# First loads over three queues and first splits held behind the front, in a conditioned short-convolution layer on one Trainium2 core

## The chip, the core and the metric

The kernel runs on one core of a Trainium2 chip. Its time is the device time of one execution in microseconds (us); lower is better. The core has TensorE (PE, with its weight loads shown as PEld), VectorE (DVE), ScalarE (ACT), GpSimd (POOL) and SyncE (SP). Each engine works through its own instructions in order. Transfers are issued by an engine's instructions onto that engine's queue and are carried by 16 DMA engines.

## The reference

One layer is computed on x of 256 tokens by 2048 features, in float32, conditioned by a vector c.

```python
h = rmsnorm(x, norm_g)                         # x * rsqrt(mean(x*x) + 1e-6) * g
mod = silu(c) @ ada_w + ada_b                  # ada_w: 2048 x 6144
shift, scale, gate = split(mod, 3)
h = h * (1 + scale) + shift
b_gate, c_gate, v, g = split(h @ w_in, 4)      # w_in: 2048 x 16384
u = causal_depthwise_conv(c_gate * v, conv_w)  # 3 taps per channel
y = (b_gate * u * silu(g)) @ w_out             # w_out: 4096 x 2048
x = x + gate * y
out = rmsnorm(x, final_g)
```

## The kernel before

Features lie on the partitions. Every large product is done in three float32r products: each operand is split into a rounded part (`hi`, a cast by ScalarE) and the remainder (`lo`, a subtraction by VectorE), and hi*hi, hi*lo and lo*hi are summed.

The program has a **front**, whose order is written out by hand (`in_order` ties each instruction to the one before it on its engine), and a **body**, which the tile framework's scheduler orders by its own timeline of the program (`schedule_with_timeline_sim=True`). Where no tie holds, the scheduler may also put instructions of the body between those of the front. That concerns above all the loads on SP's queue.

The front:

- x is loaded in four tiles of 512 KB, `x_84` and `x_85` (left and right half of the first 128 tokens), `x_86` and `x_87` (of the other 128). Four small loads bring the rows of c, norm_g, ada_b and conv_w; PE turns them into columns (`tp_v`, line 240).
- ScalarE squares the first 128 tokens (line 275), VectorE the others (line 278); from the sums comes `rstd`, with which ScalarE scales x (line 300). PE turns the scaled x (`tp_x`, line 306) and ScalarE copies it to `xs`.
- For the first two of the 16 feature tiles, shift and scale come first. `first_ada` loads their columns of ada_w, 4 MB in pieces `at` of 4, 4, 4, 2, 1 and 1 of the 16 rows of blocks (k); each piece is two transfers, one for shift and one for scale. These pieces borrow the buffers of `lo` and `hi` in turn, three of each. VectorE multiplies each k by silu(c) and adds (`gv`, lines 362 and 364), except the k in `ON_PE`, which PE sums directly (`sum0_of`, line 350). At the end PE sums `gv` over its partitions (`sum0(None, ...)`, line 350), VectorE forms `scale` and `shift` (lines 391 to 393), ScalarE and VectorE write the first two tiles of `hT` (`features`, lines 328 to 332), and the products of `raw0` (512 KB of w_in, two transfers, line 188) begin.
- `idle(n, ...)` issues `IDLE[n]` products without use on PE at fixed places of the front.

The body of the first stage runs two new feature tiles against 1 MB pieces `raw_s` of w_in (line 525, the first is 512 KB), each split by line 338 (`hi`) and line 339 (`lo`) and followed by 48 products on PE (line 466). Three buffers `raw` hold raw0 and the pieces. Between them, `ada_piece` loads the ada_w columns of the later feature tiles in pieces of two transfers of 256 KB (`at`, line 435, four buffers); a group of two feature tiles takes eight such pieces.

A load also waits for the eighth load ahead of it: the framework gives the transfers of SP and ACT eight semaphores (`DMAHW0` to `DMAHW7`) in turn, and a semaphore is used again when the transfer that had it has landed. Transfers of GpSimd have semaphores of their own.

Of the kernel before, what the change touches and what calls it, by code (L numbers as in the profile page):

```python
# [11 lines left out]
ALU = mybir.AluOpType  # L12

P = 128
# [114 lines left out]
def short_conv_layer(ctx: ExitStack, tc: tile.TileContext, x, c, norm_g, ada_w, ada_b, w_in, conv_w, w_out, final_g, out):  # L129
    nc = tc.nc  # L130
# [16 lines left out]
    def slot(shape, name, dtype=F32):  # L147
        return slots.tile(shape, dtype, tag="slot", name=name)
# [19 lines left out]
    @contextmanager  # L168
    def behind(last):

        traced = nc.cur_bb.bb.instructions
        n = len(traced)
        yield
        for ins in list(traced[n:]):
            if ins.engine in last:
                tc.add_manual_dep(ins, last[ins.engine], after, reason="behind")
# [13 lines left out]
    ended = {}  # L190
# [4 lines left out]
    rows1 = const.tile([80, P], F32, tag="rows1", name="rows1")  # L195
    rows2 = const.tile([96, P], F32, tag="rows2", name="rows2")
    HX = D // 2
    GIVE = 300
    IDLE = (20, 8, 28, 2, 6, 4, 12, 8)
    xt = [[slot([P, HX], f"x{t}{dh}") for dh in range(2)] for t in range(TT)]  # L200
    for t in range(TT):
        for dh in range(2):
            nc.sync.dma_start(xt[t][dh], x[t * P : (t + 1) * P, dh * HX : (dh + 1) * HX])  # L203
    nc.scalar.dma_start(rows1[64:80, :], c.rearrange("o (k p) -> (o k) p", p=P))
    nc.scalar.dma_start(rows1[0:16, :], norm_g.rearrange("o (k p) -> (o k) p", p=P))
    nc.scalar.dma_start(rows1[16:64, :], ada_b.rearrange("o (k p) -> (o k) p", p=P))
    nc.scalar.dma_start(rows2[:, :], conv_w.rearrange("w (k p) -> (w k) p", p=P))

    adas = ada_w[0].rearrange("(k p) (s f) -> p k s f", p=P, s=3)
    NK0 = ADA[0]
    first_ada = []
    for n, (j, kk) in enumerate(((0, 4), (4, 4), (8, 4), (12, 2), (14, 1), (15, 1))):
        at = wpool.tile([P, SLOT], F32, tag=("lo", "hi")[n % 2], name="at0", bufs=3)[:, : kk * 2 * NK0 * P]
        at = at.rearrange("p (k s f) -> p k s f", k=kk, s=2)
        if n == 0:
            wpool.tile([P, 32], F32, tag="line3", name="line3", bufs=1)
        for s in range(2):
            nc.sync.dma_start(at[:, :, s, :], adas[:, j : j + kk, s, 0 : NK0 * P])  # L220
        first_ada.extend(at[:, i] for i in range(kk))
# [3 lines left out]

    ident = const.tile([P, P], F32, tag="ident", name="ident")
    make_identity(nc, ident)
    ones_e = const.tile([P, P], F32R, tag="ones", name="ones")
    ones = ones_e.bitcast(F32)
    nc.vector.memset(ones, 1.0)  # L230
# [15 lines left out]
    turned = [psum.tile([P, CT, T], F32, tag="mm", name="tp_x") for _ in range(3)]  # L246
# [4 lines left out]
    def idle(n, where):  # L251
        for _ in range(IDLE[n]):
            nc.tensor.matmul(where[:, 0, :], ones_r[:, 0:P], ones_r[:, T:], start=True, stop=True, skip_group_check=True)
# [7 lines left out]
    gT = vec[:, 0:16]  # L261
    b_shift = vec[:, 16:32]
    b_scale1 = const.tile([P, KT], F32, tag="bsc", name="b_scale1")
# [8 lines left out]
    for t in range(TT):  # L272
        for dh in range(2):
# [3 lines left out]
            else:  # L277
                nc.vector.scalar_tensor_tensor(
                    out=junk[:, t], in0=xt[t][dh], scalar=1.0, in1=xt[t][dh], op0=ALU.mult, op1=ALU.mult,
# [16 lines left out]
    def scaled_x(j):  # L296
        c = slice(j % 2 * CT * P, (j % 2 + 1) * CT * P)
        for t in range(TT):
            xp = xt[t][j // 2][:, c]
            nc.scalar.activation(xp, xp, AF.Copy, scale=rstd[:, t : t + 1])  # L300

    def turn_x(tp, j):
        for i in range(CT):
            c = slice((j % 2 * CT + i) * P, (j % 2 * CT + i + 1) * P)
            for t in range(TT):
                nc.tensor.transpose(tp[:, i, t * P : (t + 1) * P], xt[t][j // 2][:, c], ident)

    shift = const.tile([P, KT], F32, tag="shift", name="shift")
    scale = const.tile([P, KT], F32, tag="scale", name="scale")
# [24 lines left out]
    def split(raw, n, lo_tag="lo"):  # L334

        hi = wpool.tile([P, SLOT], F32R, tag="hi", name="hi", bufs=3)
        lo = wpool.tile([P, SLOT], F32R, tag=lo_tag, name="lo", bufs=3)
        nc.scalar.copy(hi[:, :n], raw[:, :n])  # L338
        nc.vector.tensor_tensor(out=lo[:, :n], in0=raw[:, :n], in1=hi[:, :n].bitcast(F32), op=ALU.subtract)  # L339
        return hi, lo  # L340


    ON_PE = (3, 7, 11, 13)
    sums0 = psum.tile([P, 512], F32, tag="sm", name="sum0", bufs=2)
    gv0 = adap.tile([P, 2, 2 * P], F32, tag="gv", name="gv0")[:, :, 0 : NK0 * P]

    def sum0(k, rows, col):

        for o in range(2 * NK0):
            nc.tensor.matmul(  # L350
                sums0[:, o : o + 1], rows[:, o // NK0, (o % NK0) * P : (o % NK0 + 1) * P], col,
                start=k == ON_PE[0] and o == 0, stop=k is None, skip_group_check=True,
            )

    def sum0_of(n):
        k = ON_PE[n]
        sum0(k, first_ada[k], silu_c[:, k : k + 1])
# [8 lines left out]
    scaled_x(1)  # L366
    turn_x(turned[0], 0)
    nc.scalar.copy(xs[0], turned[0])
    sum0_of(0)
    scaled_x(2)  # L370
    turn_x(turned[1], 1)
    nc.scalar.copy(xs[1], turned[1])
    idle(3, turned[2])
    sum0_of(1)
    idle(4, turned[2])
    scaled_x(3)
    turn_x(turned[2], 2)
    nc.scalar.copy(xs[2], turned[2])
    turned.append(psum.tile([P, CT, T], F32, tag="mm", name="tp_x"))
    idle(5, turned[3])  # L380
    sum0_of(2)
    turn_x(turned[3], 3)
    nc.scalar.copy(xs[3], turned[3])
    sum0_of(3)
    tp_idle = psum.tile([P, CT, T], F32, tag="mm", name="tp_idle")
    idle(6, tp_idle)
    sum0(None, gv0, ones[:, 0:1])

    sums_shift, sums_scale = sums0[:, 0:NK0], sums0[:, NK0 : 2 * NK0]
    ks = slice(0, NK0)  # L390
    nc.vector.tensor_tensor(out=scale[:, ks], in0=sums_scale, in1=b_scale1[:, ks], op=ALU.add)
    nc.vector.tensor_tensor(out=scale[:, ks], in0=scale[:, ks], in1=gT[:, ks], op=ALU.mult)
    nc.vector.tensor_tensor(out=shift[:, ks], in0=sums_shift, in1=b_shift[:, ks], op=ALU.add)
    hi0 = wpool.tile([P, SLOT], F32R, tag="hi", name="hi", bufs=3)
    lo0 = wpool.tile([P, SLOT], F32R, tag="lo", name="lo", bufs=3)
    w = CT * P
    for k in range(NK0):
        nc.scalar.copy(hi0[:, k * w : (k + 1) * w], raw0[:, k * w : (k + 1) * w])
    for k in range(NK0):
        c = slice(k * w, (k + 1) * w)  # L400
        nc.vector.tensor_tensor(out=lo0[:, c], in0=raw0[:, c], in1=hi0[:, c].bitcast(F32), op=ALU.subtract)
        features(k)
    idle(7, tp_idle)
    pinned.close()
    pieces0 = [(hi0, lo0)]

# [87 lines left out]
    def keep(ch, q, k0, bank, seed=False):  # L494
# [4 lines left out]
        else:  # L499
            nc.vector.tensor_tensor(out=acc[ch, q], in0=bank, in1=acc[ch, q], op=ALU.add)  # L500

    def parts(chs, q, k0, k1, seeds, between):

        w = len(chs) * CT * P
        col = q * E + chs[0] * CT * P
        step = SLOT // w
        first = k0
        banks = []
        for ch, seed in zip(chs, seeds):
            banks.append(psum.tile([P, CT, T], F32, tag="mm", name="mm_s"))  # L510
            if seed:
                nc.scalar.copy(banks[-1], acc[ch, q])
        if pieces0:
            for k in range(NK0):
                chunk_products(banks[0], *pieces0[0], k * CT * P, k, k0, k1, late=True)
            pieces0.clear()
            k0 = NK0
            for some in between:
                for piece in some:
                    ada_piece(*piece)  # L520
        for s0, some in zip(range(k0, k1, step), between):
            sk = min(step, k1 - s0)
            n = sk * w
            raw = raw_tile("raw_s")
            nc.sync.dma_start(
                raw[:, :n].rearrange("p (k f) -> p k f", k=sk),
                w_in[0, s0 * P : (s0 + sk) * P, col : col + w].rearrange("(k p) f -> p k f", p=P),
            )
            hi, lo = split(raw, n)
            for piece in some:  # L530
                ada_piece(*piece)
            for j, (bank, seed) in enumerate(zip(banks, seeds)):
                if first == 0:
                    opening_products(bank, hi, lo, w, j * CT * P, s0, sk, k1)
                else:
                    for i in range(sk):
                        chunk_products(bank, hi, lo, i * w + j * CT * P, s0 + i, first, k1, seed)
        for ch, bank, seed in zip(chs, banks, seeds):
            keep(ch, q, first, bank, seed)
# [74 lines left out]
    for ct in range(NS, NCT, 2):  # L614
        for q in QUARTERS:
            bank = psum.tile([P, CT, T], F32, tag="mm", name="mm_b")[:, 0:2]
            col = q * E + ct * P
            for kp in range(0, KT, KP):
                raw = raw_tile("raw")
# [4 lines left out]
                hi, lo = split(raw, SLOT)  # L624
                for m in range(2):
                    for i in range(KP):
                        k = kp + i
                        o = slice((i * 2 + m) * P, (i * 2 + m + 1) * P)
# [64 lines left out]
    for dc in range(4):  # L693
# [10 lines left out]
        for ep in range(n_ep):  # L704

            first = dc == 0 and ep == 0
            raw = wpool.tile([P, SLOT], F32, tag="raw" if first else "lo", name="raw_o", bufs=3)
# [4 lines left out]
            if dc == 3:  # L712
# [3 lines left out]
                    out=raw3, in0=raw3, in1=gate(dc).unsqueeze(1).to_broadcast([P, EP, 512]), op=ALU.mult  # L716
# [57 lines left out]
```

## Time and profile before

| | |
|---|---|
| median of three runs | 913.68 us (913.65 to 915.89) |
| profiled execution, its own time | 913.47 us |
| its span, first to last instruction | 911.7 us |
| PE busy | 898.6 us, 99% of the span |
| DVE / ACT busy | 628.8 us / 451.7 us |
| bytes moved by DMA | 227.64 MB, mean 250 GB/s |
| mean granted TensorE clock | 0.999 |

The page gives busy time by engine and by groups of instructions; a query of the trace gives a stretch of it instruction by instruction (start, length, engine, line, tile, and in brackets the idle time before it and what ended that). The chain of waits follows the work that ended last back in time. SPq and ACTq are the instructions that issue transfers. PE's 99% includes the idle products, so being busy there does not by itself tell of useful work.

### The profile page before, as it was taken

How to read it: one execution, taken by the hardware profiler on the slowest of the kernel's cores; microseconds unless marked ns; L12 is line 12 of the kernel's file. 1: busy time of each engine (PE TensorE's matmuls, PEld its weight loads, DVE VectorE, ACT ScalarE, POOL GpSimd, SP SyncE). 2: the span in 40 equal slices, each digit the busy share in tenths (PEclk: the TensorE clock that was granted, in tenths of full speed). 3: DMA queues.
4: the chain of work that ended last, by engine and by line, in shares of the span. 5: the costliest groups of instructions: out<-in, count | busy, mean ns of one | idle time of the engine just before them, and what ended most of it. 6: DMA issues, size and time to landing. Idle time of an engine off the chain costs nothing.

```text
span 911.7 us, 16332 instructions
## 1 busy us (share of the span) xinstructions
PE 898.6 (99%) x7111; PEld 866.5 (95%) x7111; DVE 628.8 (69%) x605; ACT 451.7 (50%) x427; POOL 0.7 (0%) x6
## 2 busy tenths in 40 slices
PE   8999999999999999999999999999999999999997
PEld 7899999999999999999999999999999988888885
DVE  4888989999988999985555455545455544555882
ACT  6678876544545755554333443334433333443333
POOL 0000000000000000000000000000000000000000
PEclk9999999999999999999999999999999999999999
DMA  9999999999898778867666666666666496665542
GB/s 305 375 384 372 321 361 349 329 362 351 286 350 308 239 246 280 281 225 223 198 188 187 193 200 202 190 186 191 200 192 201 141 346 213 198 202 195 185 139 92
DMA packets 146791, 227.64 MB, mean 250 GB/s; under 512 B 5360, under 2 KB 103840, under 8 KB 146336
## 3 DMA queue, kind: packets, MB, share of 16 engines
q1 hardware_dynamic: 146480, 226.51, 74.0%
q8 instruction: 55, 0.90, 0.4%
q14 instruction: 16, 0.13, 0.0%
q10 hardware_dynamic: 240, 0.09, 0.0%
HBM read 224.49 MB, written 2.10 MB: 249 GB/s over the span
## 4 chain that ended last, share of the span: by engine, by line
PE 95%; DMA 3%; DVE 1%; ACT 0%; SPq 0%; issue 0%; ACTq 0%; DVEq 0%
PE mm_b L466 38%; PE mm_s L466 37%; PE mm_o L671 6%; PE mm_o L670 6%; PE mm_o L672 6%; DMA raw_s<-in_sc_w_in_dram 1%; DMA at<-in_ada_w_dram 1%; DMA x<-in_x_dram 1%; DVE gv L364 1%; PE tp_g L455 0%; ACT hi L338 0%; PE ps_gate L609 0%; SPq L220 0%; DVE lo L339 0%; PE sum L350 0%; SPq L203 0%
## 5 line engine op out<-in xcount | busy, mean ns | idle before, releaser
L466 PE MATMUL mm_b<-hT,hi 128*128 128x256 f32 x2048 | 348.4, 276 | 0.0
L466 PE MATMUL mm_s<-hT,hi 128*128 128x256 f32 x2048 | 336.6, 277 | 1.6 <-ACT hi L338 1.0
L466 PEld LDWEIGHTS mm_b<-hT,hi 128*128 128x128 f32 x2048 | 308.4, 188 | 0.0
L466 PEld LDWEIGHTS mm_s<-hT,hi 128*128 128x128 f32 x2048 | 299.4, 188 | 2.5 <-ACT hi L338 1.2
L466 PE MATMUL mm_b<-hT,lo 128*128 128x256 f32 x1024 | 282.6, 276 | 0.0
L466 PE MATMUL mm_s<-hT,lo 128*128 128x256 f32 x1024 | 262.1, 276 | 0.0
L339 DVE TENSOR_TENSOR lo<-raw,hi 128x2048 fp32r<-128x2048 f32 x64 | 146.7, 2291 | 128.2 <-ACT hi L338 128.2
L338 ACT CAST hi<-raw 128x2048 fp32r<-128x2048 f32 x64 | 122.5, 1913 | 196.3 <-PE mm_b L466 149.0
L466 PEld LDWEIGHTS mm_b<-hT,lo 128*128 128x128 f32 x1024 | 192.2, 188 | 0.1
L466 PEld LDWEIGHTS mm_s<-hT,lo 128*128 128x128 f32 x1024 | 182.8, 188 | 0.0
L338 ACT CAST hi<-raw_s 128x2048 fp32r<-128x2048 f32 (+1 forms) x64 | 121.4, 1901 | 96.6 <-PE mm_s L466 79.5
L339 DVE TENSOR_TENSOR lo<-raw_s,hi 128x2048 fp32r<-128x2048 f32 (+1 forms) x64 | 145.4, 2272 | 21.2 <-ACT hi L338 20.1
L339 DVE TENSOR_TENSOR lo<-raw_o,hi 128x2048 fp32r<-128x2048 f32 x32 | 73.3, 2290 | 64.0 <-ACT hi L338 64.0
L338 ACT CAST hi<-raw_o 128x2048 fp32r<-128x2048 f32 x32 | 61.0, 1907 | 106.7 <-PE mm_o L672 81.3
L671 PE MATMUL mm_o<-lo,y 128*128 128x512 f32 x256 | 99.3, 389 | 0.0
L672 PE MATMUL mm_o<-hi,y 128*128 128x512 f32 x256 | 99.3, 389 | 0.0
L670 PE MATMUL mm_o<-hi,y 128*128 128x512 f32 x256 | 99.3, 389 | 0.0
L448 DVE SCALAR_TENSOR_TENSOR gv<-at,silu_c,gv 128x512 f32<-128x512 f32 x105 | 78.6, 749 | 2.1 <-DMA at<-in_ada_w_dram 0.3
L672 PEld LDWEIGHTS mm_o<-hi,y 128*128 128x128 f32 x256 | 48.0, 188 | 10.0
L670 PEld LDWEIGHTS mm_o<-hi,y 128*128 128x128 f32 x256 | 48.0, 188 | 10.0
L671 PEld LDWEIGHTS mm_o<-lo,y 128*128 128x128 f32 x256 | 48.1, 188 | 9.8
L498 ACT COPY acc<-mm_s 128x1024 f32<-128x1024 f32 x43 | 43.4, 1017 | 22.7 <-PE mm_s L466 22.3
(105 smaller groups left out, 386.8 us busy)
## 6 DMA issues: line engine op xcount, KB each, us to landing
raw<-in_sc_w_in_dram SPq DMA_DIRECT2D x64, 1024.0 KB, 5.6
raw_s<-in_sc_w_in_dram SPq DMA_DIRECT2D x63, 1024.0 KB, 7.2
raw_o<-in_sc_w_out_dram SPq DMA_DIRECT2D x32, 1024.0 KB, 5.2
at<-in_ada_w_dram SPq DMA_DIRECT2D x114, 256.0 KB, 7.4
at_g<-in_ada_w_dram SPq DMA_DIRECT2D x32, 512.0 KB, 6.2
at<-in_ada_w_dram SPq DMA_DIRECT2D x6, 512.0 KB, 8.7
x<-in_x_dram SPq DMA_DIRECT2D x4, 512.0 KB, 6.3
big<-in_x_dram SPq DMA_DIRECT2D x2, 1024.0 KB, 7.7
```

The lines of the kernel that those rows point to most:

```text
L338: nc.scalar.copy(hi[:, :n], raw[:, :n])
L339: nc.vector.tensor_tensor(out=lo[:, :n], in0=raw[:, :n], in1=hi[:, :n].bitcast(F32), op=ALU.subtract)
L364: nc.vector.scalar_tensor_tensor(out=gv0, in0=first_ada[k], scalar=c_k, in1=gv0, op0=ALU.mult, op1=ALU.add)
L448: nc.vector.scalar_tensor_tensor(out=gv, in0=at4[:, i], scalar=c_k, in1=gv, op0=ALU.mult, op1=ALU.add)
L466: mm = last_mm[0] = nc.tensor.matmul(dst, w, h[:, k], start=begins and left, stop=ends, skip_group_check=True)
L498: nc.scalar.copy(acc[ch, q], bank)
L670: nc.tensor.matmul(po, yh, hi[:, o], start=opens, stop=False, skip_group_check=True)
L671: nc.tensor.matmul(po, yh, lo[:, o], start=False, stop=False, skip_group_check=True)
L672: nc.tensor.matmul(po, yl, hi[:, o], start=False, stop=ct == NCT - 1, skip_group_check=True)
```

## The change

The rows of norm_g, ada_b and conv_w are issued by GpSimd, after it has made the identity; the right halves of x (`dh` = 1) by ScalarE, behind c. `first_ada`'s third piece of four k becomes two pieces of two k, so there are seven pieces, and the last takes the buffer of the first. `ON_PE` loses k = 3, which VectorE now sums. The sums and transposes on PE stand in another order, with other counts of idle products between them. `scale` is formed per feature tile in one instruction. The hi and lo splits of the first three `raw_s` pieces are tied behind the front's last instruction on their engines.

```diff
-    IDLE = (20, 8, 28, 2, 6, 4, 12, 8)
+    IDLE = (20, 6, 12, 4, 4, 6, 7, 7, 9)
     xt = [[slot([P, HX], f"x{t}{dh}") for dh in range(2)] for t in range(TT)]
+    nc.scalar.dma_start(rows1[64:80, :], c.rearrange("o (k p) -> (o k) p", p=P))
     for t in range(TT):
         for dh in range(2):
-            nc.sync.dma_start(xt[t][dh], x[...])
-    nc.scalar.dma_start(rows1[64:80, :], c.rearrange("o (k p) -> (o k) p", p=P))
-    nc.scalar.dma_start(rows1[0:16, :], norm_g...)
-    nc.scalar.dma_start(rows1[16:64, :], ada_b...)
-    nc.scalar.dma_start(rows2[:, :], conv_w...)
+            queue = nc.scalar if dh else nc.sync
+            queue.dma_start(xt[t][dh], x[...])
...
-    for n, (j, kk) in enumerate(((0, 4), (4, 4), (8, 4), (12, 2), (14, 1), (15, 1))):
+    for n, (j, kk) in enumerate(((0, 4), (4, 4), (8, 2), (10, 2), (12, 2), (14, 1), (15, 1))):
         at = wpool.tile([P, SLOT], F32, tag=("lo", "hi")[n % 2], name="at0", bufs=3)[...]
...
     make_identity(nc, ident)
+    nc.gpsimd.dma_start(rows1[0:16, :], norm_g...)
+    nc.gpsimd.dma_start(rows1[16:64, :], ada_b...)
+    nc.gpsimd.dma_start(rows2[:, :], conv_w...)
...
-    ON_PE = (3, 7, 11, 13)
+    ON_PE = (7, 11, 13)
...
     turn_x(turned[0], 0)
     nc.scalar.copy(xs[0], turned[0])
-    sum0_of(0)
     scaled_x(2)
     turn_x(turned[1], 1)
+    idle(3, turned[2])
+    sum0_of(0)
+    scaled_x(3)
     nc.scalar.copy(xs[1], turned[1])
-    idle(3, turned[2])
-    sum0_of(1)
-    idle(4, turned[2])
-    scaled_x(3)
     turn_x(turned[2], 2)
     nc.scalar.copy(xs[2], turned[2])
     turned.append(psum.tile([P, CT, T], F32, tag="mm", name="tp_x"))
-    idle(5, turned[3])
-    sum0_of(2)
+    idle(4, turned[3])
     turn_x(turned[3], 3)
     nc.scalar.copy(xs[3], turned[3])
-    sum0_of(3)
     tp_idle = psum.tile([P, CT, T], F32, tag="mm", name="tp_idle")
+    idle(5, tp_idle)
+    sum0_of(1)
     idle(6, tp_idle)
+    sum0_of(2)
+    idle(7, tp_idle)
     sum0(None, gv0, ones[:, 0:1])
...
-    nc.vector.tensor_tensor(out=scale[:, ks], in0=sums_scale, in1=b_scale1[:, ks], op=ALU.add)
-    nc.vector.tensor_tensor(out=scale[:, ks], in0=scale[:, ks], in1=gT[:, ks], op=ALU.mult)
-    nc.vector.tensor_tensor(out=shift[:, ks], in0=sums_shift, in1=b_shift[:, ks], op=ALU.add)
+    for k in range(NK0):
+        if k == 1:
+            nc.vector.tensor_tensor(out=shift[:, 0:NK0], in0=sums0[:, 0:NK0], in1=b_shift[:, 0:NK0], op=ALU.add)
+        nc.vector.tensor_scalar(out=scale[:, k : k + 1], in0=sums0[...], scalar1=b_scale1[...], scalar2=gT[...], op0=ALU.add, op1=ALU.mult)
...
-    idle(7, tp_idle)
+    idle(8, tp_idle)
...
+    first_pieces = [None] * 3
...
-            hi, lo = split(raw, n)
+            with behind(ended if first_pieces else {}):
+                hi, lo = split(raw, n)
+            first_pieces[:] = first_pieces[1:]
```

How the instructions stand now is shown at three places. The first is SP's queue from the start of the program; `at_96` to `at_112` are the pieces of `first_ada`, `at` without a number is a half of a piece of `ada_piece`, for the second pair of feature tiles. Before:

```order
L203 DMA x_84<-in_x_dram 128x1024
L203 DMA x_85<-in_x_dram 128x1024
L203 DMA x_86<-in_x_dram 128x1024
L203 DMA x_87<-in_x_dram 128x1024
L220 DMA at_96<-in_ada_w_dram 128x4x256 x2
L220 DMA at_100<-in_ada_w_dram 128x4x256 x2
L220 DMA at_103<-in_ada_w_dram 128x4x256 x2
L220 DMA at_106<-in_ada_w_dram 128x2x256 x2
L220 DMA at_109<-in_ada_w_dram 128x256 x2
L220 DMA at_112<-in_ada_w_dram 128x256 x2
L188 DMA raw_115<-in_sc_w_in_dram 128x512 x2
L525 DMA raw_s<-in_sc_w_in_dram 128x2x512
```

In the changed kernel (`at_93` to `at_112` are now the pieces of `first_ada`):

```order
L205 DMA x_84<-in_x_dram 128x1024
L438 DMA at<-in_ada_w_dram 128x2x256
L205 DMA x_86<-in_x_dram 128x1024
L218 DMA at_93<-in_ada_w_dram 128x4x256 x2
L218 DMA at_97<-in_ada_w_dram 128x4x256 x2
L218 DMA at_100<-in_ada_w_dram 128x2x256 x2
L218 DMA at_103<-in_ada_w_dram 128x2x256 x2
L218 DMA at_106<-in_ada_w_dram 128x2x256 x2
L218 DMA at_109<-in_ada_w_dram 128x256 x2
L438 DMA at<-in_ada_w_dram 128x2x256 x7
L218 DMA at_112<-in_ada_w_dram 128x256 x2
L188 DMA raw_115<-in_sc_w_in_dram 128x512 x2
```

Two of the four x tiles have left the queue. Eight `at` of 256 KB, 2 MB that stood behind `raw_s` or later, now stand ahead of `at_112`, the last piece of `first_ada`: one between the two x tiles, seven just ahead of `at_112`.

The second place is VectorE at the end of the front, from the last sums of `gv` on. Before:

```order
L364 SCALAR_TENSOR_TENSOR gv_222<-at_109,silu_c,gv_222 128x512
L364 SCALAR_TENSOR_TENSOR gv_222<-at_112,silu_c,gv_222 128x512
L391 TENSOR_TENSOR scale<-sum_221,b_scale_162 128x2
L392 TENSOR_TENSOR scale<-scale,vec 128x2
L393 TENSOR_TENSOR shift<-sum_221,vec 128x2
L401 TENSOR_TENSOR lo<-raw_115,hi 128x512
L339 TENSOR_TENSOR lo<-raw_s,hi 128x1024
L329 TENSOR_SCALAR xs_215<-xs_215,scale,shift 128x256
L332 TENSOR_TENSOR hT<-xs_215,hT 128x256
L401 TENSOR_TENSOR lo<-raw_115,hi 128x512
```

In the changed kernel:

```order
L365 SCALAR_TENSOR_TENSOR gv_207<-at_109,silu_c,gv_207 128x512
L365 SCALAR_TENSOR_TENSOR gv_207<-at_112,silu_c,gv_207 128x512
L393 TENSOR_SCALAR scale<-sum_206,b_scale_165,vec 128x1
L392 TENSOR_TENSOR shift<-sum_206,vec 128x2
L393 TENSOR_SCALAR scale<-sum_206,b_scale_165,vec 128x1
L404 TENSOR_TENSOR lo<-raw_115,hi 128x512
L330 TENSOR_SCALAR xs_200<-xs_200,scale,shift 128x256
L333 TENSOR_TENSOR hT<-xs_200,hT 128x256
L404 TENSOR_TENSOR lo<-raw_115,hi 128x512
L330 TENSOR_SCALAR xs_200<-xs_200,scale,shift 128x256
L333 TENSOR_TENSOR hT<-xs_200,hT 128x256
L340 TENSOR_TENSOR lo<-raw_s,hi 128x1024
```

The subtraction for the first `raw_s` (128x1024) has moved from between the two parts of `raw_115` to behind the features of both tiles, and scale takes one instruction per tile.

The third is ScalarE from its last copy of x on. Before:

```order
L383 COPY xs_218<-tp_x 128x1024
L398 CAST hi<-raw_115 128x512 x2
L338 CAST hi<-raw_s 128x1024
L328 ACTIVATE hT<-xs_215,shift,scale 128x256 x2
L338 CAST hi<-raw_s 128x2048
```

In the changed kernel:

```order
L381 COPY xs_203<-tp_x 128x1024
L401 CAST hi<-raw_115 128x512 x2
L329 ACTIVATE hT<-xs_200,shift,scale 128x256 x2
L339 CAST hi<-raw_s 128x1024
L339 CAST hi<-raw_s 128x2048
```

The cast of the first `raw_s` has moved from ahead of the two `hT` to behind them.

More of the change, by code (lines that the diff above doesn't have):

```diff
@@ L198, in short_conv_layer @@
     GIVE = 300
-    IDLE = (20, 8, 28, 2, 6, 4, 12, 8)
+    IDLE = (20, 6, 12, 4, 4, 6, 7, 7, 9)
     xt = [[slot([P, HX], f"x{t}{dh}") for dh in range(2)] for t in range(TT)]
+    nc.scalar.dma_start(rows1[64:80, :], c.rearrange("o (k p) -> (o k) p", p=P))
     for t in range(TT):
         for dh in range(2):
-            nc.sync.dma_start(xt[t][dh], x[t * P : (t + 1) * P, dh * HX : (dh + 1) * HX])
-    nc.scalar.dma_start(rows1[64:80, :], c.rearrange("o (k p) -> (o k) p", p=P))
-    nc.scalar.dma_start(rows1[0:16, :], norm_g.rearrange("o (k p) -> (o k) p", p=P))
-    nc.scalar.dma_start(rows1[16:64, :], ada_b.rearrange("o (k p) -> (o k) p", p=P))
-    nc.scalar.dma_start(rows2[:, :], conv_w.rearrange("w (k p) -> (w k) p", p=P))
+            queue = nc.scalar if dh else nc.sync
+            queue.dma_start(xt[t][dh], x[t * P : (t + 1) * P, dh * HX : (dh + 1) * HX])
     adas = ada_w[0].rearrange("(k p) (s f) -> p k s f", p=P, s=3)
@@ L227, in short_conv_layer @@
     make_identity(nc, ident)
+    nc.gpsimd.dma_start(rows1[0:16, :], norm_g.rearrange("o (k p) -> (o k) p", p=P))
+    nc.gpsimd.dma_start(rows1[16:64, :], ada_b.rearrange("o (k p) -> (o k) p", p=P))
+    nc.gpsimd.dma_start(rows2[:, :], conv_w.rearrange("w (k p) -> (w k) p", p=P))
     ones_e = const.tile([P, P], F32R, tag="ones", name="ones")
@@ L379, in short_conv_layer @@
     turned.append(psum.tile([P, CT, T], F32, tag="mm", name="tp_x"))
-    idle(5, turned[3])
-    sum0_of(2)
+    idle(4, turned[3])
     turn_x(turned[3], 3)
     nc.scalar.copy(xs[3], turned[3])
-    sum0_of(3)
     tp_idle = psum.tile([P, CT, T], F32, tag="mm", name="tp_idle")
+    idle(5, tp_idle)
+    sum0_of(1)
     idle(6, tp_idle)
+    sum0_of(2)
+    idle(7, tp_idle)
     sum0(None, gv0, ones[:, 0:1])
-    sums_shift, sums_scale = sums0[:, 0:NK0], sums0[:, NK0 : 2 * NK0]
-    ks = slice(0, NK0)
-    nc.vector.tensor_tensor(out=scale[:, ks], in0=sums_scale, in1=b_scale1[:, ks], op=ALU.add)
-    nc.vector.tensor_tensor(out=scale[:, ks], in0=scale[:, ks], in1=gT[:, ks], op=ALU.mult)
-    nc.vector.tensor_tensor(out=shift[:, ks], in0=sums_shift, in1=b_shift[:, ks], op=ALU.add)
+    for k in range(NK0):
+        if k == 1:
+            nc.vector.tensor_tensor(out=shift[:, 0:NK0], in0=sums0[:, 0:NK0], in1=b_shift[:, 0:NK0], op=ALU.add)
+        nc.vector.tensor_scalar(
+            out=scale[:, k : k + 1], in0=sums0[:, NK0 + k : NK0 + k + 1], scalar1=b_scale1[:, k : k + 1],
+            scalar2=gT[:, k : k + 1], op0=ALU.add, op1=ALU.mult,
+        )
     hi0 = wpool.tile([P, SLOT], F32R, tag="hi", name="hi", bufs=3)
```

## The prediction

> **What bounds the kernel now.** I read the page's busy times first, then PE's waits, then the chain of waits up to 60 us, the timeline of the front, and the transfers.
>
> ```profile
> PE 898.6 (99%) x7111; PEld 866.5 (95%) x7111; DVE 628.8 (69%) x605; ACT 451.7 (50%) x427; POOL 0.7 (0%) x6
> ```
> ```profile
> PE tp_v L240 <- DMA rows<-in_c_dram: 4.2, 1, 4.2
> PE mm_s L466 <- ACT hi L338: 1.0, 1, 1.0
> PE mm_s L466 <- ACT hT L328: 0.4, 1, 0.4
> PE tp_x L306 <- ACT x L300: 0.3, 1, 0.3
> PE sum L350 <- DVE gv L364: 0.2, 1, 0.2
> PE mm_s L466 <- DVE hT L332: 0.2, 1, 0.2
> ```
>
> These six waits are all that PE has in the whole program: after the last one it works through to its final product. The change touches nothing behind the first stage's start. So the time moves with one number: when PE's useful products start, plus what they still wait after the start. The next rows give that number (columns of the windows: length, then busy time and count of PE, PEld, DVE, ACT and POOL, the granted clock, the DMA share, GB/s).
>
> ```profile
> 26.86:39.53 12.67, 11.47 (x96) 11.07 (x96) 10.61 (x16) 6.35 (x6) 0.00 (x0) 1.00 1.05 382
> 39.53:380.00 340.47, 340.47 (x2995) 340.16 (x2996) 308.90 (x344) 216.56 (x233) 0.00 (x0) 1.00 0.93 323
> ```
>
> From 39.53 on PE has no gap. Before that it ran 96 products in 12.67 us. The chain gives their pitch:
>
> ```profile
> 10.40 9.06 DMA at<-in_ada_w_dram
> ...
> 19.58 0.76 DVE gv L364
> ...
> 23.52 0.76 DVE gv L364
> ...
> 24.32 1.07 PE sum L350 x8
> ...
> 25.41 0.17 DVE scale L391
> ...
> 27.59 9.88 DMA raw_s<-in_sc_w_in_dram
> ...
> 39.53 16.61 PE mm_s L466 x144
> ```
>
> 144 products in 16.61 us are 0.1153 us each. 96 of them are 11.07 us, so 12.67 - 11.07 = 1.60 us were lost behind the start at 26.86. The **effective start** of before is 26.86 + 1.60 = 28.46 us. The chain says what makes it: loads of ada_w up to 19.46, six `gv` steps on VectorE, the sum on PE, scale, then a `raw_s` piece that landed late (37.47) and its cast. VectorE's `gv`, six steps in a row, was late there, not the last load:
>
> ```profile
> 16.44 0.33 SPq L220 DMA_DIRECT2D at<-in_ada_w_dram  x1
> ```
> ```profile
> at<-in_ada_w_dram SPq DMA_DIRECT2D x1, 128.0 KB, 6.0
> ```
>
> The second half of `at_112`, the last `first_ada` piece, was issued at 16.44 and landed 6.0 us later, at 22.44; its `gv` began at 23.52.
>
> **The change, part by part.**
>
> *SP's queue.* This carries the forecast. The order of instructions has eight `at` of 256 KB ahead of `at_112`, that is 2 MB that before came behind it. Bytes ahead of the end of `at_112` were 2 MB of x and 4 MB of `first_ada`; now they are 8 MB. What a MB costs there: the chain's `at` load landed at 10.40 + 9.06 = 19.46; it was the second half of `at_103`, the end of the third MB of `first_ada`. The fourth MB ended at 22.44, 2.98 us later. The rate in between, and its two exceptions:
>
> ```profile
> 6.00:8.00 2.00, 2.00 (x12) 2.00 (x11) 0.00 (x0) 1.96 (x4) 0.00 (x0) 1.00 0.91 265
> 8.00:10.00 2.00, 2.00 (x14) 1.80 (x13) 0.93 (x1) 0.43 (x2) 0.00 (x0) 1.00 1.04 393
> 18.00:20.00 2.00, 2.00 (x20) 2.00 (x19) 1.26 (x3) 1.98 (x4) 0.00 (x0) 1.00 1.11 349
> 26.00:28.00 2.00, 1.56 (x13) 1.34 (x11) 1.97 (x4) 1.31 (x3) 0.00 (x0) 1.00 1.01 404
> ```
>
> 349 GB/s is 3.0 us for a MB of ada_w, which agrees; the DMA engines are full at it (share 1.11). Two MB are then 6.0 us, and `at_112` lands at 22.44 + 6.0 = 28.45. That is the upper end. The lower: with x on two queues the dip at 6 to 8 us may fill; at 393 instead of 265 GB/s those 2 us would carry 0.26 MB more, worth 0.7 us, so 27.7. I take 28.1, the middle, since nothing shows the dip's cause.
>
> [...]
>
> *The front's end, from `at_112` on.* Its `gv` is the only step left by then (below), so the backlog of six steps is gone: 0.12 from landing to start (19.46 to 19.58) and 0.80 to the sum (23.52 to 24.32). The sum to scale is 25.41 - 24.32 = 1.09. The rest needs these rows:
>
> ```profile
> 25.26 1.05 ACT L338 CAST hi<-raw_s 128x1024 fp32r<-128x1024 f32 x1 [0.88 <-DMA at<-in_ada_w_dram]
> 26.22 1.09 ACT L328 ACTIVATE hT<-xs,shift,scale 128x256 fp32r<-128x256 f32 x2
> ```
> ```profile
> 25.68 0.15 DVE L393 TENSOR_TENSOR shift<-sum,vec 128x2 f32<-128x2 f32 x1
> ```
> ```profile
> 26.86 0.74 PE L466 MATMUL mm_s<-hT,hi 128*128 128x256 f32 x4 [0.44 <-ACT hT L328]
> ```
>
> Shift was ready at 25.83, but `hT` began at 26.22, behind the cast of `raw_s`. That cast now comes behind `hT`: 0.39 saved. One dependent step of scale goes: about 0.1. So scale's start to `hT` is 0.30 where it was 0.81, and `hT` to the first product stays 26.86 - 26.22 = 0.64. Together 0.12 + 0.80 + 1.09 + 0.30 + 0.64 = 2.95 us behind the landing of `at_112`: the first product starts at 31.05.
>
> *What PE then still waits.* The `lo` of `raw_s` no longer stands on VectorE ahead of the low part of `hT`, for which PE waited 0.2; with the gaps around it I leave 0.2. The wait of 1.0 for `hi` at 39.53 goes: the `raw_s` of the chain, the third piece, has 11 MB up to its end in both orders (6 + 0.5 + 0.5 + 0.5 + 1 + 1.5 + 1 before, 8 + 0.5 + 0.5 + 2 now), while PE comes to it later. It is issued when `raw0` is split, some 2 us behind the first product; with half of the 9.88 us that it took behind other loads, and a cast, it is there 9 us behind the first product. PE has 96 products, 11 us, ahead of it. So the effective start is 31.05 + 0.2 = 31.25, and the change 31.25 - 28.46 = **+2.8 us**.
>
> *Off the path.* Sharing the DMA engines between two queues, x_84 and x_85 move side by side, and x_86 has 256 KB ahead of it. Rows: the last square, the last copy of x, and the landing of conv_w's rows by ScalarE's queue.
>
> ```profile
> 10.53 1.23 DVE L278 SCALAR_TENSOR_TENSOR junk<-x 128x1024 f32<-128x1024 f32 x1 [0.23 <-DMA x<-in_x_dram]
> ```
> ```profile
> 21.82 1.01 ACT L383 COPY xs<-tp_x 128x1024 f32<-128x1024 f32 x1 [1.18 <-PE tp_x L306]
> ```
> ```profile
> DMA to landing us min/median/max: 7.4/7.4/7.4
> ```
>
> The last x tile could land from 2 us earlier to 1.5 us later than 10.4. The copies of x end at 22.83 today; at worst at some 25, well ahead of 28.1. VectorE's `gv`, now with k = 3 (0.76 more), ends its first fifteen steps by about 24, so it waits for `at_112`. The same 4 us cover everything else that is moved: the rows by GpSimd (busy 0.7 us in the whole program; a transfer of rows by its queue isn't in the trace, I bound it by ScalarE's 7.4 us for conv_w's rows and twice that; the first is hidden, the second is a rival below); two fewer issues on SP and one fewer on ACT; two more on SP for the piece that is cut in two; the sum of k = 3 that PE no longer makes. `at_112` waits for the `gv` of `at_93`, some 17 us in, and for its semaphore, about 22 (estimates at the same pace): the second binds and is the queue's own pace. The idle products, 88 before and 75 now, stand in time when PE waits for loads.
>
> *Sum.* 913.47 + 2.8 = **916.3 us**. The profiled execution lies 0.2 below the median of the runs shown (913.68), and its span of 911.7 leaves 1.8 around it, which I leave as it is.
>
> **Rivals.**
>
> *The pieces cost nothing, since the rate rises* (the other side). If x on two queues and the order after it let the front run at the 404 GB/s of 26 to 28 us, the 5.75 MB behind x take 14.9 us instead of 17.3 and x itself ends a us earlier: `at_112` at 24.7, start at 27.9, **912.9**. It is faster than before from a landing under 25.3 on. Against it: that rate is w_in's with longer rows, and ada_w's stays at 349 for 12 us with full DMA engines. A landing of 26.5 would be the half way, 914.7.
>
> *PE falls to its slow pace in the wait.* PE has nothing to do between its last idle products and the final sum:
>
> ```profile
> 4.41 4.52 PE L253 MATMUL tp_x<-ones_r 128*128 128x256 f32 x20
> ...
> 19.90 0.95 PE L350 MATMUL sum<-silu_c,at 128*128 128x1 f32 x8
> 20.71 1.07 PE L306 MATMUL tp_x<-ident,x 128*128 128x128 f32 x8
> ```
>
> After the 4.2 us wait at the program's start, 20 idle products took 4.52 us, 0.226 each. At 0.1153 they take 2.31, so a start from the slow pace costs 2.2 us, of which the nine idle products ahead of the first useful one cover a part: 1 to 2 us on top, **917.9**. It takes a wait about as long as that at the start. PE's last turn of x ended at 21.78; behind it now stand 20 idle products (2.3 us) and two sums (0.95 each), so PE is done at 26, or at 24 to 27.5 as x lands, and the final sum starts at 28.1 + 0.92 = 29.0: a wait of 1.5 to 5 us. Before, no wait behind 4.2 us was over 1.0, so the trace doesn't show where the limit is. The granted clock says 1.00 throughout and doesn't show this pace. [...]
>
> *Rows by GpSimd come late.* PE's turn of the rows stands ahead of all of x, in order. The 4 us of slack are used up if the rows land behind some 14 us, and each us beyond costs a us: at 17 us, **919**. The first of the two bounds is far from it, the second touches it.
>
> **How the numbers follow.** The forecast's own range is a landing of 27.3 to 28.6, 915.3 to 916.9: chance 0.50. Higher rate, 912.0 to 915.3: 0.25. The slow pace, 916.9 to 919.3: 0.17. Late rows, or a wait in the body that the new order of loads makes: 0.05, above 919. Below 912: 0.03. The range leaves out the two last and the lowest part of the rate's case: 913.4 to 919.2. What can be told from no change is 0.3%, 2.7 us here, so slower begins at 916.4: somewhat under half of the forecast's case, and the two above it, 0.45; same 0.51; faster (under 910.9) 0.04.
>
> **What would show it.** Right: `at_112` lands at 27.5 to 28.6, VectorE waits 3 to 5 us for it, the first product at 30.5 to 31.5 with `hT` right behind shift, and no wait of PE over 0.3 behind that; the `hi` wait at 39.5 is gone. Wrong: `at_112` before 26; useful products at 0.2 us each at first (slow pace); PE waiting behind 35 us; PE's turn of the rows waiting for GpSimd's transfers.

## The result and the profile after

| | before | after |
|---|---|---|
| median of six executions on the same chip | 913.86 us (913.55 to 915.89) | 919.08 us (918.54 to 919.85) |
| ratio, 95% interval | | 1.0053 (1.0040 to 1.0066) |
| span of the profiled execution | 911.7 us | 917.2 us |
| mean granted TensorE clock | 0.999 | 0.992 |

The kernel is 5.2 us slower. PE's waits of the whole program after the change:

```profile
PE tp_v L241 <- DMA rows<-in_c_dram: 4.3, 1, 4.3
PE tp_x L307 <- ACT x L301: 3.5, 2, 3.2
PE sum L351 <- DVE gv L365: 2.8, 1, 2.8
```

The waits for `hi` and `hT` behind the start are gone. One wait of 2.8 us, for the last `gv`, stands in front of the start. The wait for the scaled x (3.5 us, 0.3 before) is new too: x is scaled from 14.11 us on instead of 12.77, and 18 fewer idle products stand ahead of it. PE was still done with its list at 26.60, before the last `gv` ended at 29.31, so this wait does not set the start. The chain of waits up to 60 us says what it hangs on:

```profile
8.64 8.71 DMA at<-in_ada_w_dram
...
17.37 5.25 DMA at<-in_ada_w_dram
...
22.64 5.79 DMA at<-in_ada_w_dram
...
28.55 0.76 DVE gv L365
...
29.35 1.87 PE sum L351 x8
31.22 2.13 PE tp_idle L254 x9
33.35 26.70 PE mm_s L469 x225
```

Before, loads ended in this chain at 19.46 and six steps of `gv` followed. Now loads of ada_w fill it to 28.43, with a single `gv` behind. What SP issued ahead of that last load (timeline of SP's queue):

```profile
17.37 4.63 SPq L438 DMA_DIRECT2D at<-in_ada_w_dram  x7
22.12 0.87 SPq L218 DMA_DIRECT2D at<-in_ada_w_dram  x2
```

The seven `at` of line 438, for the next pair of feature tiles, went out first, and `at_112` (line 218) behind them at 22.12 to 22.99. `gv` waited 5.41 us on VectorE for it:

```profile
28.55 0.75 DVE L365 SCALAR_TENSOR_TENSOR gv<-at,silu_c,gv 128x512 f32<-128x512 f32 x1 [5.41 <-DMA at<-in_ada_w_dram]
```

The other half of the loss is in PE's own rows (PE's timeline, then the windows, with the granted clock third from the end):

```profile
25.52 1.08 PE L254 MATMUL tp_idle<-ones_r 128*128 128x256 f32 x7
29.35 1.87 PE L351 MATMUL sum<-ones,gv 128*128 128x1 f32 x8 [2.76 <-DVE gv L365]
31.08 2.27 PE L254 MATMUL tp_idle<-ones_r 128*128 128x256 f32 x9
33.15 1.05 PE L469 MATMUL mm_s<-hT,hi 128*128 128x256 f32 x4
```
```profile
14.00:16.00 2.00, 0.83 (x4) 0.64 (x5) 1.93 (x4) 1.89 (x4) 0.00 (x0) 0.82 1.10 348
...
18.00:20.00 2.00, 2.00 (x17) 2.00 (x16) 1.92 (x3) 2.00 (x4) 0.00 (x0) 0.83 1.10 346
...
28.00:30.00 2.00, 0.65 (x3) 0.65 (x4) 0.75 (x1) 0.79 (x2) 0.00 (x0) 0.73 1.06 397
30.00:32.00 2.00, 2.00 (x10) 2.00 (x11) 0.74 (x4) 0.71 (x2) 0.00 (x0) 0.50 0.95 379
32.00:34.00 2.00, 2.00 (x11) 2.00 (x10) 1.97 (x5) 2.00 (x4) 0.00 (x0) 0.50 0.09 37
34.00:36.00 2.00, 2.00 (x12) 2.00 (x12) 1.97 (x4) 1.65 (x1) 0.00 (x0) 0.56 0.48 92
```

The clock is 0.50 from about 28.9 to 35.8 us (and once earlier in this execution, from 15.3 to 18.7, after the wait for x). In the two windows from 30 to 34 us, at half clock, PE is busy for all of the 2 us, but with 10 and 11 instructions; the window from 18 to 20 us before the change, at full clock, holds 20. The eight small products of the final sum took 1.87 us (1.07 before the change), and the nine idle ones 2.27. The first product starts at 33.15. The 225 products of the chain end at 33.35 + 26.70 = 60.05; at 0.1153 each they take 25.94, so the effective start is 60.05 - 25.94 = 34.11. Before, it was 28.46, so it is 5.6 us later, and the spans differ by 5.5. Next to nothing is left to explain behind the front.

### The profile page after: what moved, and what is told of

It reads as the page before. It is cut to its first block, busy times and chain, and to the rows that moved or that the text cites. A ratio compares the mean times of both kernels' runs of the same rounds, so it can differ in the third digit from the quotient of the medians.

```text
span 917.2 us, 16302 instructions
## 1 busy us (share of the span) xinstructions
PE 899.6 (98%) x7090; PEld 868.2 (95%) x7090; DVE 628.8 (69%) x606; ACT 452.0 (49%) x427; POOL 2.3 (0%) x9
## 4 chain that ended last, share of the span: by engine, by line
PE 96%; DMA 3%; ACT 0%; DVE 0%; ACTq 0%; issue 0%; SPq 0%; DVEq 0%
PE mm_s L469 38%; PE mm_b L469 38%; PE mm_o L678 6%; PE mm_o L679 6%; PE mm_o L677 6%; DMA at<-in_ada_w_dram 3%; PE tp_g L458 0%; PE tp_idle L254 0%; PE sum L351 0%; PE ps_gate L616 0%; DVE gv L365 0%; ACT big L691 0%; ACT big L688 0%; ACTq L777 0%; SPq L205 0%
```

## The experiments

Two questions: is the late landing of `at_112` the cause, and which part of the change makes it late; and how much does the half clock add. The ratio is each kernel against the kernel before, with its 95% interval.

**The cut undone.** The changed kernel, with the third piece whole again:

```diff
-    ... ((0, 4), (4, 4), (8, 2), (10, 2), (12, 2), (14, 1), (15, 1))
+    ... ((0, 4), (4, 4), (8, 4), (12, 2), (14, 1), (15, 1))
```

> The changed kernel with the third piece of first_ada in one (4 k, as before), so six pieces and no reuse of the first one's buffer. In the order of instructions seven of the eight at loads then go back behind raw_s; one stays between the x tiles. Theory: the last piece lands at 23.2 (22.4 and one load of 0.75), and PE's own list, which ended at 26.6 in the changed kernel, sets the final sum: first product at about 28.7, 914.0 or a little less, 5 us less than the changed kernel. Rival, the x tiles on two queues or the rows by GpSimd are what costs: 918 to 919.

Measured: 914.36 us, ratio 1.0011 (1.0002 to 1.0020). With six pieces the seven `at` of line 438 stand behind the first `raw_s`. PE no longer waits for the sum:

```profile
28.30 0.95 PE L351 MATMUL sum<-ones,gv 128*128 128x1 f32 x8
...
30.39 0.72 PE L469 MATMUL mm_s<-hT,hi 128*128 128x256 f32 x4
```

The sum comes without a wait, so here PE's own list of sums and idle products sets it; VectorE's last `gv` had ended at 24.24. The list is late in this execution (915.97 us, 1.6 above the median), since the clock was at half from about 16.8 to 23.6 us (0.69, 0.50, 0.50 and 0.60 in the four windows from 16 to 24 us). One edit takes the loss from 0.53% to 0.11%, four fifths of it.

**The loads held back instead.** The changed kernel, with the seven pieces, but the `at` of the next pair tied behind the front's last instruction on their queue:

```diff
-            nc.sync.dma_start(at4[:, :, s, :], ...)
+            with behind(ended if k0 == ADA[0] else {}):
+                nc.sync.dma_start(at4[:, :, s, :], ...)
```

> The changed kernel with the loads of the first later group tied behind the front's last load on SP, so all eight at loads stand behind raw0 and the seven pieces stay. Theory: at_112 lands at 22.5 to 23 (its buffer is free at about 17), PE's list sets the final sum at 26.6, 914.0 as in the run with six pieces. Rival, the seventh piece costs by itself, through the wait for its buffer: 916 or more.

Measured: 913.62 us, ratio 0.9998 (0.9990 to 1.0007). PE's rows, its largest wait behind the start, and the load in the chain that goes with it:

```profile
23.87 0.95 PE L351 MATMUL sum<-ones,gv 128*128 128x1 f32 x8
...
25.96 0.74 PE L470 MATMUL mm_s<-hT,hi 128*128 128x256 f32 x4
```
```profile
PE mm_s L470 <- ACT hi L339: 1.1, 2, 0.6
```
```profile
27.47 8.98 DMA raw_s<-in_sc_w_in_dram
```

With all the other edits in place and only the order of the loads mended, the first product is 0.9 us earlier than before (26.86), and waits for `raw_s` give that back.

**The cut alone.** The kernel before, with nothing but the third piece cut in two:

```diff
-    ... ((0, 4), (4, 4), (8, 4), (12, 2), (14, 1), (15, 1))
+    ... ((0, 4), (4, 4), (8, 2), (10, 2), (12, 2), (14, 1), (15, 1))
```

> The kernel before with one edit of the change: the third piece of first_ada cut in two, so that the seventh piece waits for the first one's buffer. Its order of instructions then has all eight at loads of the next group ahead of the last piece. Theory: the last piece lands at 28.4, PE's wait for the final sum is over 3 us and its pace falls: 918.5 to 919.5. Rival, the harm needs the other edits (two queues for x, splits held back): 914.

Measured: 919.95 us, ratio 1.0069 (1.0056 to 1.0082). All eight `at` stand ahead of the last piece here, and the chain and PE's waits show the same picture as the changed kernel:

```profile
24.29 5.10 DMA at<-in_ada_w_dram
...
30.32 1.87 PE sum L350 x8
```
```profile
PE sum L350 <- DVE gv L364: 6.1, 1, 6.1
```

This one edit does the whole harm by itself. The three runs together settle the first question: the loads ahead of `at_112` are the cause, and the cut puts them there. Why it does is read from the order of instructions, not measured by itself: the first six pieces have a buffer each, the seventh must wait until VectorE has used the first, and the scheduler put loads that were ready into that place of the queue.

**x on one queue.** The changed kernel, with all four tiles of x on SP:

```diff
-            queue = nc.scalar if dh else nc.sync
+            queue = nc.sync
```

> The changed kernel with all of x on SP's queue again; its order still has eight at loads ahead of at_112, now in one row. Theory: the same bytes are ahead, at_112 lands at 28.4 and PE goes slow again: 919, within 0.5. Rival, x on ScalarE's queue makes x and with it the front late: 917 or less.

Measured: 919.46 us, ratio 1.0064 (1.0052 to 1.0077). `at_112` ends the loads of the chain at 29.01:

```profile
24.14 4.87 DMA at<-in_ada_w_dram
```

The split of x is not the cause; without it the landing is 0.6 us later.

**The wait filled, first try.** The changed kernel with idle products up to the final sum:

```diff
-    IDLE = (20, 6, 12, 4, 4, 6, 7, 7, 9)
+    IDLE = (20, 6, 12, 4, 4, 6, 7, 31, 9)
```

> The changed kernel with 24 more idle products ahead of the final sum (2.8 us at 0.1153), and nothing else. Theory: of the 5.5 us, some 3 are the late landing of at_112 (28.4 instead of 22.4) and some 2.5 are PE's slow pace from 28.9 to 35.8. With PE kept busy to the final sum the clock stays at full speed, at_112 still lands at 28.4, and the first product comes 2.95 behind it at 31.4: about 2.5 us less than the changed kernel, 916.5. Rival, the slow pace costs nothing since PE waits for data anyway: 919, no change.

Measured: 919.27 us, ratio 1.0058 (1.0045 to 1.0071): a miss in the time. The clock was 1.00 in all windows from 20 to 60 us and the start came earlier. But the trace also shows the body in another order than the changed kernel's (on VectorE from 36.8 us on), and a new wait of 1.6 us at 322 us (PE's timeline and waits):

```profile
29.59 1.05 PE L351 MATMUL sum<-ones,gv 128*128 128x1 f32 x8 [0.34 <-DVE gv L365]
...
31.78 0.72 PE L469 MATMUL mm_s<-hT,hi 128*128 128x256 f32 x4
```
```profile
PE mm_s L469 <- DVE acc L503: 1.6, 1, 1.6
```

The next two runs have the same order as this one and no such wait, so the order alone does not make it; what does stays open. The run therefore shows the front with the clock at 1.00, its first product 1.37 us earlier than in the changed kernel, and nothing on the whole.

**The wait filled, second try.** With 20 for the 12 as well, which was meant to leave every other instruction in the order of the changed kernel:

```diff
-    IDLE = (20, 6, 12, 4, 4, 6, 7, 7, 9)
+    IDLE = (20, 6, 20, 4, 4, 6, 7, 31, 9)
```

> The changed kernel with 8 more idle products in the early gap of PE (11.7 to 14.9) and 24 more ahead of the final sum; unlike in the first run of this kind, every other instruction stands as in the changed kernel on all engines. Theory: clock 1.00 from the final sum on, first product at 31.5, no wait of PE behind it, so the 2.2 us that the first of these runs gained at the front are not given back in the body: 916.7, 2.2 to 2.6 under the changed kernel. Rival, the body gives back whatever the front gains: 919.

Measured: 917.86 us, ratio 1.0046 (1.0034 to 1.0058). The premise did not hold: in the traces, PE (without its idle products), VectorE, ScalarE and SP have the order of the run before, not that of the changed kernel. PE has no wait behind the start here.

```profile
29.50 1.05 PE L351 MATMUL sum<-ones,gv 128*128 128x1 f32 x8
...
31.68 0.74 PE L469 MATMUL mm_s<-hT,hi 128*128 128x256 f32 x4
```
```profile
30.00:32.00 2.00, 2.00 (x16) 1.83 (x17) 1.41 (x5) 1.49 (x3) 0.00 (x0) 1.00 0.99 398
```
```profile
31.72 28.37 PE mm_s L469 x247
```

The sum begins 0.15 us later than in the changed kernel and the first product 1.47 earlier. The effective start is 31.72 + 28.37 - 247 x 0.1153 = 31.61, 3.15 later than before; the profiled span is 914.8, 3.1 longer than before and 2.4 shorter than that of the changed kernel. The whole executions differ by less: the profiled one took 918.04 us, 0.95 under the changed kernel's 918.99, and the two ratios are 0.0007 apart, some 0.6 us, with intervals that overlap. The other executions of this kernel had spans of 915.7 to 916.4, and what they lost was not traced. So the half clock is shown as a loss at the front, 34.11 - 31.61 = 2.5 us of the effective start in the traced executions. How much of it the whole kernel loses is not shown: the orders of the two bodies differ, and the times do not separate. Nor is the landing's part exact: by the ratio, the kernel with the full clock is still 4.2 us slower than before, where its trace explains 3.1.

**The wait halved.** With 14 instead of 7 in that place of the changed kernel, to shorten the idle stretch by 0.8 us (the order is that of the two runs before here too):

```diff
-    IDLE = (20, 6, 12, 4, 4, 6, 7, 7, 9)
+    IDLE = (20, 6, 12, 4, 4, 6, 7, 14, 9)
```

> The changed kernel with 7 more idle products ahead of the final sum (14 for 7), all else as there. PE's wait for the sum shrinks from 2.8 to some 1.9 us. If the pace falls when a stretch of 3.41 us (the spacing that the clock's changes keep) is mostly idle, this one is over half busy. Then the clock may stay: 916.7. If any wait of about 2 us is enough: 919, as the changed kernel.

Measured: 919.08 us, ratio 1.0063 (1.0047 to 1.0079), single executions from 917.53 to 921.64. In the profiled one PE still waited 2.69 us, since its list stood 0.7 us earlier in that execution. The clock fell at about 31.5, 2.6 us later than in the changed kernel:

```profile
30.00:32.00 2.00, 2.00 (x15) 1.84 (x15) 1.46 (x5) 1.51 (x4) 0.00 (x0) 0.87 0.86 342
32.00:34.00 2.00, 2.00 (x11) 2.00 (x11) 1.93 (x6) 1.20 (x3) 0.00 (x0) 0.50 0.04 16
```

PE was busy again from 29.44, and the clock was still at half from 2 us later on, for one stretch of 3.4 us (it was 0.78 from 34 to 36 and 1.00 behind that) instead of 6.8. So two waits of about the same length, 2.76 and 2.69 us, were followed by a fall at different places (28.9 and 31.5 us) and of different length. With the same order and on the same chip, the median is 1.2 us above that of the run before; the intervals overlap. The run does not tell a limit for the wait, since the wait was hardly shorter.

**The useful part of the change alone, loads tied.** The kernel before, with the seven pieces, the one-step scale, the splits behind the front, and each `at` of the next pair tied behind the `raw_s` load that the code has ahead of it, and six idle products fewer ahead of the sum:

```diff
-    IDLE = (20, 8, 28, 2, 6, 4, 12, 8)
+    IDLE = (20, 8, 28, 2, 6, 4, 6, 8)
...
-            nc.sync.dma_start(at4[:, :, s, :], ...)
+            with behind(last_raw if k0 == NK0 else {}):
+                nc.sync.dma_start(at4[:, :, s, :], ...)
```

> The kernel before with the parts of the change that shorten the front, and SP's queue held in the order of the code: seven pieces, scale in one instruction, the first three splits behind the front, 6 idle products fewer ahead of the final sum, x and rows as before; each at load of the first later group is tied behind the raw_s load that the code has ahead of it. Theory: the last piece lands at 22.4, its gv ends at 23.6 instead of 24.3, the first product comes at 25.7, the third raw_s lands by 35 instead of 37.5, and the effective start is 25.9 to 26.5: 911 to 911.6, if the scheduler puts no new wait into the body. Rival, the front is bound by the bytes up to the third raw_s, whatever the order: 913.5.

Measured: 913.77 us, ratio 0.9999 (0.9988 to 1.0011), single executions from 911.31 (clock 0.999) to 916.40 (0.995).

```profile
22.33 0.96 PE L253 MATMUL tp_idle<-ones_r 128*128 128x256 f32 x6
23.57 1.05 PE L350 MATMUL sum<-ones,gv 128*128 128x1 f32 x8 [0.28 <-DVE gv L364]
...
26.34 1.05 PE L472 MATMUL mm_s<-hT,hi 128*128 128x256 f32 x4
```
```profile
24.00:26.00 2.00, 2.00 (x13) 2.00 (x13) 1.33 (x5) 1.08 (x3) 0.00 (x0) 0.62 1.09 374
26.00:28.00 2.00, 2.00 (x12) 2.00 (x12) 1.93 (x6) 1.13 (x2) 0.00 (x0) 0.52 1.01 397
```

The sum starts 0.75 us earlier than before (24.32). But the clock is at half from about 24.5 to 27.9, though PE waited only 0.28 us ahead of it. The median misses the expected 911 to 911.6; the lowest executions reach it.

**The same with more idle products.** 12 ahead of the sum again, and then 10 ahead of it and 12 behind it:

```diff
-    IDLE = (20, 8, 28, 2, 6, 4, 6, 8)
+    IDLE = (20, 8, 28, 2, 6, 4, 12, 8)     # and (20, 8, 28, 2, 6, 4, 10, 12)
```

> As the kernel with loads tied behind raw_s, with 12 idle products ahead of the final sum (as before the change) where it had 6. If its slow pace came from too few streaming products in the stretch ahead (theory: PE counts as busy by its columns, not by having no wait), it now stays at full pace in nearly all executions: the sum some 0.2 us later, and the spread from 911.3 to 916.4 closes to 911.4 to 912.2, median 911.8, ratio 0.998. Rival: the pace depends on where the end of PE's list falls on the clock's grid and not on the idle products; then the spread stays, median 913.8.

> The same with 10 idle products ahead of the final sum and 12 (for 8) behind it. By the theory the pace stays full, as with 12 and 8; the 12 behind the sum end at about the time hT is ready (24.5 + 1.4 = 25.9 against 26.2), so they delay nothing: 911.7. Rival: the products behind the sum delay the first useful one by up to 0.4 us, 912.2; or the spread stays, 913.8.

Measured: 912.75 us, ratio 0.9991 (0.9983 to 1.0000), from 912.12 to 914.75; and 912.58 us, ratio 0.9993 (0.9982 to 1.0003), from 911.52 to 915.50. In both profiled fronts the clock was 1.00 in every window from 16 to 34 us. For the second:

```profile
23.62 1.03 PE L350 MATMUL sum<-ones,gv 128*128 128x1 f32 x8
...
26.02 0.64 PE L472 MATMUL mm_s<-hT,hi 128*128 128x256 f32 x4
```

The ratios are 0.0008 and 0.0006 lower than with six idle products, some 0.7 and 0.5 us, in the direction that was expected. But the intervals overlap, neither ratio lies clearly below 1, the spread did not close, and both medians miss the expected 911.8 and 911.7. Single executions still show clocks of 0.994 to 0.996. This is the best version that the study has; that it beats the kernel before is not shown.

**The splits behind the front alone.** The kernel before with this one edit:

```diff
-            hi, lo = split(raw, n)
+            with behind(ended if first_pieces else {}):
+                hi, lo = split(raw, n)
+            first_pieces[:] = first_pieces[1:]
```

> The kernel before with one part of the change alone: the splits of the first three raw_s pieces tied behind the front. By the prediction's steps hT is 0.39 us earlier, since the cast of raw_s stood ahead of it, and the 0.2 us for the low part of hT go; the wait of 1.0 us for hi at 39.5 stays, since the loads are as before. So 0.4 to 0.6 us less: 913.3. Rival: the later split gives its buffer back later, the third raw_s piece lands later, and the wait for hi grows by as much as the start gains: 913.9 or above.

Measured: 915.32 us, ratio 1.0010 (1.0001 to 1.0019). The first product comes 0.27 us earlier, at 26.59, and the wait for `hi` doubles (PE's waits, then ScalarE's timeline):

```profile
PE mm_s L466 <- ACT hi L338: 2.0, 1, 2.0
```
```profile
37.47 1.02 ACT L498 COPY acc<-mm_s 128x1024 f32<-128x1024 f32 x1 [3.24 <-PE mm_s L466]
38.38 1.90 ACT L338 CAST hi<-raw_s 128x2048 fp32r<-128x2048 f32 x1
```

The rival was right in the outcome, not in the way: the third `raw_s` was issued at 28.13 and landed 9.4 us later, at 37.5 as before. What stands ahead of the cast now is a copy of `acc`, which waited for PE's products. That copy ends at 38.49; before, the cast began at 37.58, ahead of that copy. Behind the wait the clock was 0.91 on the mean from 42 to 60 us (1.00 before).

## Why the prediction was right or wrong

*The landing of `at_112`*: forecast 28.1, between 27.7 and 28.45; measured 22.64 + 5.79 = 28.43. The price of the 2 MB was right, and the upper bound was the better value. I gave half weight to a filled dip at 6 to 8 us. It was filled, but the stretches around it carried less. One row each, after and before, of the first 14 us:

```profile
0.00:14.00 14.00, 7.29 (x41) 6.83 (x41) 3.66 (x13) 5.43 (x9) 2.35 (x9) 1.00 0.89 289
```
```profile
0.00:14.00 14.00, 9.66 (x60) 9.25 (x60) 4.20 (x13) 6.67 (x11) 0.70 (x6) 1.00 0.86 283
```

That is 0.08 MB more and not 0.26: the 14 us had 289 GB/s with x on two queues and 283 with x on one.

*From the landing to the sum*: 0.92 forecast, 29.35 - 28.43 = 0.92 measured.

*From the sum to the first product*: 1.09 + 0.30 + 0.64 = 2.03 forecast, 33.15 - 29.35 = 3.80 measured. This is the step that failed. At full clock it was 31.68 - 29.50 = 2.18, as the second run with the wait filled shows. At half clock the sum takes 0.8 more, and the nine idle products stand in front of the first useful one: `hT` began at 31.70, 0.44 behind the start of scale instead of 0.30, and the product came 1.45 later instead of 0.64.

```profile
31.70 1.09 ACT L329 ACTIVATE hT<-xs,shift,scale 128x256 fp32r<-128x256 f32 x2 [1.29 <-DVE shift L392]
```

*What PE then still loses*: 0.2 forecast, 34.11 - 33.15 = 0.96 measured, the first products at half clock. The four terms add up: 0.33 + 0 + 1.77 + 0.76 = 2.86, which is 34.11 - 31.25.

*The slow pace* was named as a rival with 0.17 and left out of the sum. Its price, 1 to 2 us, was somewhat low for the front (2.5 traced). What was wrong is its condition, "a wait about as long as that at the start", 4.2 us, which was my estimate: here the clock was 0.50 behind a wait of 2.76 us. How long a wait it takes, no run shows. PE was done with its list at 26.60, inside the 24 to 27.5 that I gave, but partly by chance. The list itself ran at half clock for 3.4 us from 15.3 on, which the forecast did not have; at full clock it would have ended 1.7 us earlier (half of the 3.4, an estimate), and the wait would have been some 4.4 us. The forecast's 916.3 with the 2.86 us above is 919.2, against 919.08 measured. The range held it because it reached over this case, and by little: its upper end is 919.2, and one of the six executions took 919.85. The number itself was 2.8 us low.

*The rest*: the wait for `hi` at 39.5 is gone and no wait of PE stands behind the start; `hT` starts right behind shift. The sign of the slow pace is there: the first useful products took 0.21 us each (33.15 to 34.00 for four). VectorE had twelve steps ahead of `at_112`, not the fifteen that I counted; they ended at 23.14, and it then waited 5.41 us, over the 3 to 5 that I gave. The rows by GpSimd were not late; those of conv_w landed 7.0 us after their issue, against 7.4 by ScalarE's queue before (transfers):

```profile
rows<-in_sc_conv_w_dram POOLq DMA_DIRECT2D x1, 48.0 KB, 7.0
```

The rate of the loads did not rise (346 to 350 GB/s from 14 to 26 us), so the rival on the other side did not come.

## What to carry to other kernels

When a load is cut into more pieces than there are buffers, look at what the queue holds ahead of the last piece: here it became 2 MB of later loads, and bytes divided by the traced rate gave the delay to 0.3 us. When a chain of transfers moves the start, put the pace of PE behind the new gap into the sum, not beside it, with every small or idle product between the wait and the first useful one: here the clock was 0.50 from 28.92 to 35.76 us, and the sum and the nine idle products took 3.80 us up to the first useful one, where the forecast had 2.03. Three runs that differ from the changed kernel in counts of idle products alone have another order of the body in their traces, and two of them were taken to have the same. So compare the order, in the traces too, before a difference in time is put down to the pace.

## What the runs showed of the hardware

In the traced execution of the changed kernel the granted clock was 0.50 from 15.28 to 18.68 us and from 28.92 to 35.76 us, and 1.00 from 18.68 to 28.92 and from 35.76 to 60 us. The four changes lie 3.40, 10.24 and 6.84 us apart. In the experiment with six idle products the windows (0.62 from 24 to 26 us, 0.52 from 26 to 28, 1.00 ahead and behind) give one stretch from 24.48 to 27.92, 3.44 us long: an estimate, with 1.00 and 0.50 as its only two values. The 3.41 us that I used as a spacing in the expectation for the wait halved are a third of the 10.24 here. These are lengths in two executions; a rule behind them, such as the grid that another expectation names, is not shown.

The fall at 28.92 came though PE had not been idle throughout. In the 3.43 us ahead of it PE was busy for 1.09, and in the 3.41 us behind it for 2.99, with the clock at 0.50 for 3.42 us more:

```profile
25.50:28.93 3.43, 1.09 (x9) 0.89 (x8) 0.39 (x1) 0.00 (x0) 0.00 (x0) 1.00 1.07 371
28.93:32.34 3.41, 2.99 (x14) 2.99 (x15) 1.45 (x6) 1.84 (x4) 0.00 (x0) 0.50 0.93 363
```

Of those 2.99 us, 1.7 are the sum's products of a single column. In the experiment with six idle products PE had waited 0.28 us, and two sums of one column filled some 1.7 of the last 3 us ahead of the fall at 24.48. In the changed kernel the stretch from 22.10 to 25.51 held two such sums too, 1.6 us together, without a wait, and the clock there was 1.00. That PE counts as busy by its columns, the theory of the expectation for 12 idle products, was my guess; no run measured it. With 12, and with 10 and 12, the clock was 1.00 from 16 to 34 us in the two traced executions.
